# Winograd-style 3x3 convolution on one core: the first pair of images loaded by one transfer of 64 rows in place of two of 18 and 46

## The chip, the cores and the metric

The kernel runs on one core of a Trainium2 chip. The core's engines are TensorE (PE in the profile, with its weight loads as PEld), VectorE (DVE), ScalarE (ACT), GpSimd (POOL) and SyncE (SP); transfers between device memory and the on-chip memories run on 16 DMA engines that all queues share. The metric is the device time in microseconds; lower is better. It is the time of the whole kernel, from launch to the last byte stored.

## What is computed

The reference is a 3x3 convolution with padding 1 on 16 images of 64 channels and 64x64 pixels, to 128 channels, in float32:

```python
x_pad = np.pad(x, ((0, 0), (0, 0), (1, 1), (1, 1)))
for b in range(16):
    for co in range(128):
        for ci in range(64):
            for kh in range(3):
                for kw in range(3):
                    output[b, co] += weight[co, ci, kh, kw] * x_pad[b, ci, kh:kh+64, kw:kw+64]
```

The input has 16 MiB (16.8 MB), the output 32 MiB (33.6 MB).

## The kernel before, in words

Two images make a *pair*: their 2 x 64 channels fill the 128 partitions. There are eight pairs (`p`), and each is worked on in four blocks (`blk`) of eight row pairs. The kernel uses a trick along the height: for each pair of rows it needs the sum of the two input rows (`ss`, made by `sums` at L69), and the rows themselves in float16 (`xs`). In `group` (L142) TensorE accumulates in PSUM three results for each block, each for the two images (`b2`): `U`, from `ss` with the weights `G1`; `A`, from the odd rows and the row above, with the combined weights `G21` and `G0`; and `Bt`, from the even rows and the row below, with `G01` and `G2`. `U` is copied to SBUF by ACT (L156, tile `ut`); DVE adds it to `A` for the even output rows (L166) and to `Bt` for the odd output rows (L169) of the output tile `ot`. A block is 6 matmuls for `U` and 24 for `A` and `Bt`. PSUM has eight buffers of the tag `acc`, and a block takes six of them.

The loads go by three ways. SP issues, in this order and all at the start, the weights (L42), the first pair `x0` in float32 (two transfers, L46) and pairs 1 to 3 in float32 (`xf`, L50). These are on one queue, so their bytes flow in that order. POOL issues the loads of pairs 4 to 7 (L60), which convert to float16 on the way; the load of pair 4 comes after POOL's weight work (L88, L89), the others as buffers of `xs` come free.

The first pair is prepared like this (L91 to L93): in a loop over four cuts of its rows, DVE makes 8 of the 32 row sums per step (L69), and ACT casts 18, 16, 16 and 14 rows to float16 (L93). `keep` holds these instructions in program order on their engines, so DVE runs the four sums ahead of its first L166, and ACT the four casts ahead of its first L156. For the later pairs POOL makes the sums and ACT the casts (L161, pairs 1 to 3), a pair ahead of use.

The weights go another way: w_raw lands, POOL casts it (L54), TensorE transposes it by 18 small matmuls (L86), ACT copies the results to `Wt` (L87), and POOL makes the two combined weights (L88, L89).

The output tile of each image is stored whole, 2048 KB, at the end of its pair: that of the first image by SP's queue, that of the second by ACT's (held back in program order behind the next block's `ut` copies). The last pair alone is stored in two halves per image (L170), so that eighteen stores make up the output. `x0`, `xf` and `ot` share a pool of eight buffers.

Of the kernel before, what the change touches and what calls it, by code (L numbers as in the profile page):

```python
# [13 lines left out]
def kernel(  # L14
# [6 lines left out]
    nc = tc.nc  # L21
# [7 lines left out]
    x_rows = x.rearrange("b c h w -> (b c) h w")  # L29
# [12 lines left out]
    nc.sync.dma_start(w_raw, w_flat)  # L42
    x0 = opool.tile([128, H, W], F32, tag="ot", name="x0")
    cuts = [(0, 18), (18, 34), (34, 50), (50, 64)]
    for lo, hi in ((0, 18), (18, 64)):
        nc.sync.dma_start(x0[:, lo:hi, :], x_rows[0:128, lo:hi, :])  # L46
    xf = {}
    for p in (1, 2, 3):
        xf[p] = opool.tile([128, H, W], F32, tag="ot", name="xf")
# [53 lines left out]
    for p in range(NP):  # L103
# [8 lines left out]
        for blk in range(4):  # L112
# [58 lines left out]
            if blk in parts:  # L171
                lo, hi = parts[blk]
# [34 lines left out]
```

## Time and profile before

| what | value |
|---|---|
| three timed runs | 126.34, 126.49, 126.95 us (median 126.49) |
| the profiled execution's own time | 126.43 us |
| its span, from the first to the last instruction | 124.6 us |
| what lies around the span | 1.8 us |
| PE busy | 106.7 us, 86% of the span |
| DVE, ACT, POOL busy | 82.7, 51.9, 36.7 us |
| bytes moved by the DMA engines | 46.57 MB, mean 374 GB/s |
| read from device memory, written to it | 17.07 MB, 33.55 MB |

Times inside the profile are microseconds from the start of the span; an entry "7.92 4.91" starts at 7.92 and lasts 4.91. A group of instructions stands as line, engine, operation, output and inputs, and count. A DMA issue stands with its size and with the time from issue to landing. "SPq" and "ACTq" are the issues of transfers on SP's and on ACT's queue. The granted clock (PEclk) is 1.00 until the matmuls have ended. "DMA share" is the mean busy share of the 16 DMA engines; packets are booked where they start, so it can be a little over 1. A loading transfer that converts is counted in GB/s by the float16 bytes, half of those that it reads.

### The profile page before, as it was taken

To read this page: it belongs to the slowest core of one execution; us is meant where nothing else is said; L and a number is where in the kernel's file an instruction comes from. 1 tells how busy PE (TensorE), PEld (TensorE's weight loads), DVE (VectorE), ACT (ScalarE), POOL (GpSimd) and SP (SyncE) were. 2 spreads that over 40 slices of the span, in tenths; PEclk is the share of its full clock that TensorE was granted. 3 is DMA by queue.
4 is the path that set the end of the run, shared out by engine and by line. 5 is a ranking of instruction groups with operands and counts; after the bars stand their busy time and mean duration, and the time that the engine had idled before them with its cause. 6 is when DMAs were issued, how large, how long until landed. Compare 5 with 4: busy or idle time off the path is not lost.

```text
span 124.6 us, 2417 instructions
## 1 busy us (share of the span) xinstructions
PE 106.7 (86%) x978; PEld 57.5 (46%) x978; DVE 82.7 (66%) x132; ACT 51.9 (42%) x84; POOL 36.7 (29%) x27
## 2 busy tenths in 40 slices
PE   0489999999999999999999999999999999990000
PEld 0334555555555555555555555555555555540000
DVE  0016887877787787888777778777877787774000
ACT  4339569735983389333333333333333333330000
POOL 2280095195899103910058000850000000000000
PEclk9999999999999999999999999999999999999555
DMA  4999999999999999999999999999999999999992
GB/s 117 356 437 418 305 329 331 431 347 426 410 368 318 342 358 392 350 342 344 373 365 358 334 342 400 452 421 426 421 426 436 431 421 442 426 410 410 439 407 87
DMA packets 4042, 46.57 MB, mean 374 GB/s; under 512 B 448, under 2 KB 448, under 8 KB 704
## 3 DMA queue, kind: packets, MB, share of 16 engines
q1 hardware_dynamic: 2160, 25.46, 49.5%
q10 hardware_dynamic: 1296, 16.78, 31.7%
q0 software_dynamic: 576, 4.19, 16.1%
q8 instruction: 7, 0.11, 0.3%
q14 instruction: 3, 0.02, 0.0%
HBM read 17.07 MB, written 33.55 MB: 406 GB/s over the span
## 4 chain that ended last, share of the span: by engine, by line
PE 84%; DMA 4%; DVE 2%; issue 1%; DVEq 0%; SPq 0%
PE acc L142 84%; DMA x<-in_x_dram 4%; DVE ot L166 1%; DVE ss L69 1%; DVE ot L169 0%; DVEq L202 0%; SPq L42 0%; DVEq L166 0%
## 5 line engine op out<-in xcount | busy, mean ns | idle before, releaser
L142 PE MATMUL acc<-xs,Wt 64*128 64x504 f16 (+3 forms) x768 | 89.8, 380 | 0.0
L142 PEld LDWEIGHTS <-Wt 64*128 64x128 f16 x960 | 56.4, 96 | 49.8 <-issue 4.0
L156 ACT COPY ut<-acc 128x512 f32<-128x512 f32 x64 | 34.4, 589 | 53.0 <-issue 32.1
L166 DVE TENSOR_TENSOR ot<-acc,ut 128x512 f32<-128x512 f32 x64 | 41.2, 686 | 22.0 <-PE acc L142 18.2
L169 DVE TENSOR_TENSOR ot<-acc,ut 128x512 f32<-128x512 f32 x64 | 41.1, 684 | 0.0
L142 PE MATMUL acc<-ss,Wt 64*128 64x504 f16 (+1 forms) x192 | 27.2, 384 | 1.0 <-DVE ss L69 1.0
L69 POOL TENSOR_TENSOR ss<-xs 128x1024 f16<-128x1024 f16 x8 | 16.8, 2127 | 20.8 <-DMA xs<-in_x_dram 20.8
L69 POOL TENSOR_TENSOR ss<-xf 128x1024 f16<-128x1024 f32 x6 | 14.1, 2360 | 12.8 <-DMA xf<-in_x_dram 12.8
L161 ACT CAST xs<-xf 128x1024 f16<-128x1024 f32 x12 | 12.0, 1057 | 0.0
L69 DVE TENSOR_TENSOR ss<-x 128x512 f16<-128x512 f32 x4 | 2.6, 690 | 8.8 <-DMA x<-in_x_dram 8.8
L86 PE MATMUL wp<-ident,w 128*64 128x128 f16 x18 | 1.3, 328 | 4.4 <-POOL w L54 4.4
L93 ACT CAST xs<-x 128x1024 f16<-128x1024 f32 (+2 forms) x4 | 4.0, 1048 | 2.1 <-DMA x<-in_x_dram 2.1
L60 POOL DMA_DIRECT2D xs<-in_x_dram x4 | 2.4, 601 | 7.6 <-PE acc L142 7.6
L86 PEld LDWEIGHTS <-w 128*64 128x64 f16 x18 | 1.1, 209 | 4.4 <-POOL w L54 4.4
L87 ACT CAST Wt<-wp 128x384 f16<-128x384 f32 x3 | 1.2, 487 | 3.1 <-PE wp L86 3.1
L88 POOL TENSOR_TENSOR Wt<-Wt 128x384 f16<-128x384 f16 x1 | 1.4, 1387 | 1.7 <-ACT Wt L87 1.7
L87 ACT ACT_TABLE_LOAD x1 | 1.3, 1283 | 0.7 <-PEq L191 0.7
L54 POOL CAST w<-w_raw 128x576 f16<-128x576 f32 x1 | 0.7, 663 | 2.4 <-DMA w_raw<-in_weight_dram 2.4
L89 POOL TENSOR_TENSOR Wt<-Wt 128x384 f16<-128x384 f16 x1 | 0.9, 904 | 0.0
masks.py:199 POOL TENSOR_SCALAR_AFFINE_SELECT ident<-ident 128x128 f16<-128x128 f16 x1 | 0.3, 292 | 0.1
masks.py:197 POOL MEMSET ident<- 128x128 f16 x1 | 0.2, 204 | 0.3 <-POOLq L191 0.3
L191 POOL MEMSET const-float32-0.0<- 128x1 f32 x1 | 0.1, 98 | 0.2 <-issue 0.2
(3 smaller groups left out, 0.3 us busy)
## 6 DMA issues: line engine op xcount, KB each, us to landing
out_dram<-ot SPq DMA_DIRECT2D x7, 2048.0 KB, 22.3
out_dram<-ot ACTq DMA_DIRECT2D x7, 2048.0 KB, 18.5
xf<-in_x_dram SPq DMA_DIRECT2D x3, 2048.0 KB, 21.8
xs<-in_x_dram POOLq DMA_DIRECT2D x4, 1024.0 KB, 23.6
out_dram<-ot SPq DMA_DIRECT2D x2, 1024.0 KB, 11.3
out_dram<-ot ACTq DMA_DIRECT2D x2, 1024.0 KB, 11.2
x<-in_x_dram SPq DMA_DIRECT2D x1, 1472.0 KB, 7.8
x<-in_x_dram SPq DMA_DIRECT2D x1, 576.0 KB, 4.8
```

Source lines behind the costliest of these rows:

```text
L60: keep(nc.gpsimd.dma_start(xs[p], x_rows[128 * p : 128 * p + 128, :, :]))
L69: eng.tensor_add(ss[p][:, lo : lo + n, :], v[:, lo : lo + n, 0, :], v[:, lo : lo + n, 1, :])
L86: nc.tensor.matmul(wp[q : q + 64, k * CO : k * CO + CO], w16[:, t::9], ident)
L87: keep(nc.scalar.copy(wrow(g), wp[:, 0 : 3 * CO]))
L88: keep(nc.gpsimd.tensor_sub(wrow(G21), wrow(G2), wrow(G1)))
L89: keep(nc.gpsimd.tensor_sub(wrow(G01), wrow(G0), wrow(G1)))
L93: keep(nc.scalar.copy(xs[0][:, lo:hi, :], x0[:, lo:hi, :]))
L142: nc.tensor.matmul(tiles[b2][:, lo - j0 : hi - j0, c_lo:c_hi], Wt[p0 : p0 + 64, wi, kw, :], rhs, start=i == 0, stop=i == n - 1,)
L156: keep(nc.scalar.copy(ut, U[b2]))
L161: keep(nc.scalar.copy(xs[q][:, lo : lo + 16, :], xf[q][:, lo : lo + 16, :]))
L166: nc.vector.tensor_add(ots[b2][:, j0 : j0 + RB, 0, :], A[b2], us[b2])
L169: nc.vector.tensor_add(ots[b2][:, j0 : j0 + RB, 1, :], Bt[b2], us[b2])
```

## The change

The two transfers that load `x0`, of rows 0 to 17 and of rows 18 to 63, become one of all 64 rows. Nothing else is changed; the sums and casts of the first pair stay cut in four as before, but every one of them now waits for the one transfer. Behind the change all line numbers are smaller by one.

```diff
     nc.sync.dma_start(w_raw, w_flat)
     x0 = opool.tile([128, H, W], F32, tag="ot", name="x0")
     cuts = [(0, 18), (18, 34), (34, 50), (50, 64)]
-    for lo, hi in ((0, 18), (18, 64)):
-        nc.sync.dma_start(x0[:, lo:hi, :], x_rows[0:128, lo:hi, :])
+    nc.sync.dma_start(x0, x_rows[0:128, :, :])
     xf = {}
```

The engines' instructions are the same and in the same order; SP alone has one transfer fewer to issue (8,192 KB of loads in four transfers rather than five, behind the weights).

## The prediction

> **What bounds the kernel now.** I read the page first, for shares and the slices, then the chain that ended last, then the timeline of the first 16 us, then the transfers.
>
> ```profile
> span 124.6 us, 2417 instructions
> PE   0489999999999999999999999999999999990000
> DMA  4999999999999999999999999999999999999992
> PE 84%; DMA 4%; DVE 2%; issue 1%; DVEq 0%; SPq 0%
> ```
>
> Two resources are busy from end to end. PE works from slice 2 to slice 36, and the DMA engines from the start to the end. The chain, in order of time:
>
> ```profile
> 1.17 4.75 DMA x<-in_x_dram
> 5.95 0.70 DVE ss L69
> 6.69 104.25 PE acc L142 x948
> 112.28 0.59 DVEq L202
> 112.88 0.60 DVE ot L169
> ```
>
> By this chain the small first transfer of x0 (landed at 1.17 + 4.8 = 5.97) releases the first sum, that releases PE, and PE runs without a break to 110.9. But the chain stops at 113.5, and the span goes on for 11.1 us. In these only stores run, so the DMA queue has to be looked at for itself. First the busy share of the DMA engines and GB/s, the last two columns, in stretches of the span; then transfers by size and time to landing: the two of x0, the two stores of pair 5 (issued at 87.30 on SP, 87.90 on ACT), and the last store (issued at 113.51).
>
> ```profile
> 0.00:2.00 2.00, 0.00 (x0) 0.00 (x0) 0.00 (x0) 1.27 (x1) 0.70 (x6) 1.00 0.14 23
> 8.00:10.00 2.00, 2.00 (x14) 0.86 (x12) 0.55 (x1) 0.55 (x1) 0.92 (x2) 1.00 1.04 443
> 80.00:100.00 20.00, 20.00 (x190) 10.84 (x188) 15.79 (x27) 6.44 (x12) 2.64 (x2) 1.00 1.01 430
> 100.00:112.00 12.00, 12.00 (x114) 6.38 (x110) 9.24 (x16) 4.29 (x8) 0.00 (x0) 1.00 1.01 427
> 120.00:122.00 2.00, 0.00 (x0) 0.00 (x0) 0.00 (x0) 0.00 (x0) 0.00 (x0) 0.50 0.83 352
> 122.00:124.00 2.00, 0.00 (x0) 0.00 (x0) 0.00 (x0) 0.00 (x0) 0.00 (x0) 0.50 0.20 82
> ```
>
> ```profile
> x<-in_x_dram SPq DMA_DIRECT2D x1, 1472.0 KB, 7.8
> x<-in_x_dram SPq DMA_DIRECT2D x1, 576.0 KB, 4.8
> out_dram<-ot SPq DMA_DIRECT2D x1, 2048.0 KB, 16.8
> out_dram<-ot ACTq DMA_DIRECT2D x1, 2048.0 KB, 16.0
> out_dram<-ot ACTq DMA_DIRECT2D x1, 1024.0 KB, 10.2
> ```
>
> Pair 5's stores land at 104.1 and 103.9, though pair 6's are issued at 100.10 and 100.71. So when new stores come, old ones still fill the engines: the true bound is the DMA queue, and PE runs a few us ahead of it. What a later PE costs is what is over this backlog.
>
> **The change part by part.**
>
> *One issue fewer on SP.* An issue of x0 takes 0.42 us. The three xf issues behind it come that much earlier, but their bytes queue behind x0's: nothing, and if that cover were gone, a gain of 0.42.
>
> *Landing of x0.* The first use waits for 2048 KB instead of 576. Not later than the second transfer lands now, 1.6 + 7.8 = 9.4 (DVE and ACT take it at 9.46 and 9.45): the same bytes behind the same weights. Not earlier than 2.10 MB at the best rate, 443 GB/s, after the weights landed (0.73 + 2.9 = 3.6): 3.6 + 4.7 = 8.35. The 576 KB took 5.97 - 3.6 = 2.35 us, 251 GB/s, the 1472 KB 3.45 us, 437 GB/s; the slowness of the first part is either its short rows or the start itself, which the trace does not part. I take the middle, 8.9. The first sum moves from 5.95 to 8.9, so the first U matmul from 6.69 to 9.6: **2.95 us later** (2.4 to 3.5).
>
> ```profile
> 6.69 1.47 PE L142 MATMUL acc<-ss,Wt 64*128 64x512 f16 x6 [0.96 <-DVE ss L69]
> 7.92 4.91 PE L142 MATMUL acc<-xs,Wt 64*128 64x512 f16 x24
> 9.45 2.83 ACT L93 CAST xs<-x 128x1024 f16<-128x1024 f32 x3 [2.08 <-DMA x<-in_x_dram]
> 12.19 1.06 ACT L156 COPY ut<-acc 128x512 f32<-128x512 f32 x2
> 13.30 2.78 PE L142 MATMUL acc<-xs,Wt 64*128 64x512 f16 x24
> ```
>
> *What is queued behind the wait.* ACT: first cast 8.9 to 10.1 (1.17 us), the others (2.83) to 12.9, then the first L156, at 12.9 instead of 12.19. PE needs the first cut for A after U, at 9.6 + 1.3 = 10.9, and it is there at 10.1. DVE: four sums of 0.69 to 11.7, its first L166 after the ut copy, at 13.5 instead of 12.80. PE goes on meanwhile: block 0 takes six PSUM buffers, the next U the last two, and block 0 ends on PE only near 15.5. So ACT and DVE lose 0.7 us of a slack that stays; nothing of it reaches PE. POOL's weight work and its load of pair 4 (8.22) do not wait for x0. Cover gone (an eviction that holds PE): 0.7 more.
>
> *PE's slow start.* The first block takes 12.65 - 6.69 = 5.96 us, the next 15.89 - 12.65 = 3.24, at the same granted clock of 1.00; the first 24 matmuls on xs take 4.91 against 2.78. No wait explains it: PE has no idle time there. The loss is 2.72 us, and what ends it decides what the delay is worth. If the slow stretch belongs to the first block, it moves along: 2.95. If it ended at about 12.4 whatever PE did, only 12.4 - 9.6 = 2.8 us would be slow instead of 5.7, half of the difference saved: 2.95 - 1.45 = 1.5. If the transposes at 4.42 had helped it to an end and now, after a break of 3.9 us instead of 0.96, no longer do, it lasts 12.4 - 4.42 = 8.0 us from 9.6 and costs 1.15 more: 4.1. I take the first, the nearest to what the rows show, and keep 1.5 to 4.1.
>
> [...]
>
> *What the backlog takes.* PE, DVE and the store issues move by S = 2.95. For each store: had the queue been empty, how early could the end be? For pair 6's (100.10), 8192 KB of stores are left, 8.39 MB at 428 GB/s, the rate of the windows from 80 to 112: 19.6 us. From issue to data lie 1.0 us (weights issued at 0.73; a share of 0.14 in the first 2 us means data from 1.72). The tail, from the mean engine's end to the last landing at 113.51 + 10.2 = 123.7, is 1.6 now (shares after 120 add up to 2.06 us, so the mean engine ends at 122.1); after a pause that lets all 16 engines start together it may be 0.6. So the end is 100.10 + S + 1.0 + 19.6 + 0.6 to 1.6 = 121.3 to 122.3 + S, and the backlog absorbs 1.4 to 2.4 us. The landing of pair 5 bounds it from above: 104.0 - 101.1 = 2.9. I take 2.1. The stores of pair 0 (23.26) have more cover: the third xf lands at 31.4 now, and 2.10 MB of it at 430 GB/s after the second one's 24.3 last until 29.2, against 23.26 + 2.95 + 1.0 = 27.2. Load 6 must now wait for PE (pair 1 ends near 38 instead of 35.1, against an issue at 36.23), some 2 us; it lands at 36.23 + 27.4 = 63.6 now, and PE begins pair 6 at 86.3, with POOL's 4.2 us of sums between: covered by 18 us.
>
> *Sum.* 2.95 - 2.1 = +0.85 on the profiled 126.43: 127.3. The median of the runs shown, 126.49, is 0.06 above that execution; the forecast for the median is **127.3 us**, +0.7%, and its own range 126.7 to 128.4 (S from 2.4 to 3.5 with 2.1, and 2.95 with 1.4 and 2.9, and some of both).
>
> **Rivals.**
>
> 1. *Hidden.* The slow stretch ends at the old time (S = 1.5), or the backlog holds 2.9. Then DMA remains the bound everywhere; the time is 126.0 to 126.8. For it: the DMA share near 1 in every window. Against: the stretch followed PE's work in the only view there is.
> 2. *It passes in full.* If each store needs its successor early (the engines end pair 5 unevenly, and the fast ones idle from 101 on), or S is 4.1, the end moves by 2.0 to 4.1: 128.5 to 130.5, about 129.4 with S = 2.95 and no cover. Against: pair 5 landing 4 us after pair 6's issue.
> 3. *Faster.* One long transfer fills the queue's front better: x0 in 4.7 us instead of 2.35 + 3.45 = 5.8, so the whole DMA chain is 1.1 us shorter at most, 125.4, and half of that likely, 125.9. It decides only if S stays under about 1.3, since the end by the stores is 121.8 + S against 123.7 - 0.6. Against: 8.9 - 5.95 alone is 2.95.
>
> **How the numbers follow.** Forecast 0.58, hidden 0.22, in full 0.12, faster 0.08. A measurement of this kernel can tell about 0.5%, 0.63 us, from no change. Slower by more: most of the forecast (0.48; the rest of it lies within) and all of rival 2: 0.60. Faster by more: the better half of rival 3 and a little of rival 1: 0.08. Within: 0.32. The range, 125.9 to 128.9, takes in rival 1, the better part of rival 2 and the likely half of rival 3.
>
> **What would show it.** Right: one x transfer of 2048 KB landing near 8.5 to 9; the first L142 near 9.6 instead of 6.69; every later store issue later by about 2.95 (pair 6's near 103); a gap in the DMA share just before that, about 102 to 104; a time from last matmul to end shorter than now by 2. Wrong: store issues late by 3 with no gap (backlog larger), or a first block much shorter than 5.96 (rival 1), or much longer (rival 2).

## The result and the profile after

The changed kernel took 127.57 us (median of 22 runs) against 126.58 us for the kernel before beside it (22 runs). The ratio of the comparison is 1.0042, with a 95% interval of 1.0023 to 1.0062: slower, by less than the 0.5% that the prediction took as its bound, though the interval reaches past that. The changed kernel's times spread from 126.26 to 128.59, where those of the kernel before lie between 126.22 and 127.08; the ratio leaves out runs over 1.5% above a kernel's fastest, here six of the changed one, while the medians hold them all and stand 0.99 us (0.8%) apart. Two later comparisons on other chips gave 1.0083 [1.0049, 1.0118] (medians 128.26 and 126.80) and 1.0043 [1.0003, 1.0082] (medians 127.69 and 126.62).

The profiled execution of the changed kernel took 128.37 us, 0.8 above the median, so what it shows need not hold in full for the median execution; its span is 126.6 us. Its chain, in order of time (start, duration):

```profile
1.17 7.60 DMA x<-in_x_dram
8.80 0.70 DVE ss L68
9.55 103.26 PE acc L141 x948
114.16 0.60 DVEq L201
114.75 0.60 DVE ot L168
```

The one transfer of x0 lands at 8.77, the first sum starts at 8.80 instead of 5.95, and the first U matmul at 9.55 instead of 6.69: 2.86 us later. But PE's piece is 103.26 us long and not 104.25, so PE ends only 1.9 us later. The timeline of the start says where the 0.99 went:

```profile
8.80 3.88 ACT L92 CAST xs<-x 128x1152 f16<-128x1152 f32 x4 [2.59 <-DMA x<-in_x_dram]
9.55 1.47 PE L141 MATMUL acc<-ss,Wt 64*128 64x512 f16 x6 [3.92 <-DVE ss L68]
10.78 3.92 PE L141 MATMUL acc<-xs,Wt 64*128 64x512 f16 x24
12.59 1.06 ACT L155 COPY ut<-acc 128x512 f32<-128x512 f32 x2
14.52 0.83 PE L141 MATMUL acc<-ss,Wt 64*128 64x512 f16 x6
102.58 0.34 ACTq L97 DMA_DIRECT2D out_dram<-ot  x1
```

Block 0 takes 14.52 - 9.55 = 4.97 us on PE instead of 5.96: the slow stretch at PE's start ended earlier. The last line is the issue of pair 6's second store, at 102.58 instead of 100.71. In the kernel before the same line is:

```profile
100.71 0.34 ACTq L98 DMA_DIRECT2D out_dram<-ot  x1
```

So the shift that the stores see is S = 1.87 us. The DMA engines, in stretches (the last two columns are the mean busy share of the 16 engines, and GB/s):

```profile
100.00:102.00 2.00, 2.00 (x22) 1.16 (x20) 1.94 (x4) 0.10 (x1) 0.00 (x0) 1.00 0.67 279
102.00:104.00 2.00, 2.00 (x24) 1.09 (x20) 1.42 (x3) 0.97 (x2) 0.00 (x0) 1.00 0.75 320
104.00:106.00 2.00, 2.00 (x22) 1.10 (x20) 1.66 (x3) 0.93 (x2) 0.00 (x0) 1.00 1.14 483
122.00:124.00 2.00, 0.00 (x0) 0.00 (x0) 0.00 (x0) 0.00 (x0) 0.00 (x0) 0.50 0.32 135
124.00:126.00 2.00, 0.00 (x0) 0.00 (x0) 0.00 (x0) 0.00 (x0) 0.00 (x0) 0.50 0.04 16
```

The same stretches of the kernel before:

```profile
100.00:102.00 2.00, 2.00 (x22) 1.16 (x20) 1.42 (x4) 1.07 (x2) 0.00 (x0) 1.00 1.00 418
102.00:104.00 2.00, 2.00 (x22) 1.04 (x18) 1.79 (x3) 0.80 (x2) 0.00 (x0) 1.00 1.00 426
```

There the share between 100 and 104 was 1.00. Now the engines pause for 0.33 x 2 + 0.25 x 2 = 1.2 us on average, just before pair 6's stores begin to flow: the backlog of stores has run out. That is the gap that was forecast. Its place holds; what the end of the span shows (a share of 0.04 in the last window) was not forecast, and is taken up below.

### The profile page after: what moved, and what is told of

Read it like the earlier page. It is cut to its first block, busy times and chain, and to the rows that moved or that the text cites. A ratio compares the mean times of both kernels' runs of the same rounds, so it can differ in the third digit from the quotient of the medians.

```text
span 126.6 us, 2416 instructions
## 1 busy us (share of the span) xinstructions
PE 105.8 (84%) x978; PEld 57.2 (45%) x978; DVE 82.7 (65%) x132; ACT 52.0 (41%) x84; POOL 36.2 (29%) x27
## 4 chain that ended last, share of the span: by engine, by line
PE 82%; DMA 6%; DVE 2%; issue 1%; DVEq 0%; SPq 0%
PE acc L141 82%; DMA x<-in_x_dram 6%; DVE ot L165 1%; DVE ss L68 1%; DVE ot L168 0%; DVEq L201 0%; SPq L42 0%; DVEq L165 0%
## 5 line engine op out<-in xcount | busy, mean ns | idle before, releaser
L141 PE MATMUL acc<-xs,Wt 64*128 64x504 f16 (+3 forms) x768 | 88.8, 377 | 0.0
L165 DVE TENSOR_TENSOR ot<-acc,ut 128x512 f32<-128x512 f32 x64 | 41.2, 686 | 23.8 <-PE acc L141 21.5
```

Source lines behind the costliest of these rows:

```text
L141: nc.tensor.matmul(tiles[b2][:, lo - j0 : hi - j0, c_lo:c_hi], Wt[p0 : p0 + 64, wi, kw, :], rhs, start=i == 0, stop=i == n - 1,)
L165: nc.vector.tensor_add(ots[b2][:, j0 : j0 + RB, 0, :], A[b2], us[b2])
```

## The experiments

Two readings of each profile carry them: S, the issue of pair 6's second store less 100.71, and the time from that issue to the end of the span. In the table, "block 0" is PE's time from its first U to its second; S is the shift of the first U plus the change of block 0 (and, where matmuls are left out, those), to within 0.15 us. Each row shows one profiled execution; its time can lie above or below the median beside it.

| kernel | first U | block 0 | S | span | issue to end | median, us | kernel before beside it |
|---|---|---|---|---|---|---|---|
| before | 6.69 | 5.96 | 0 | 124.6 | 23.9 | 126.58 | - |
| before, less PE work | 7.37 | 5.41 | -1.35 | 124.8 | 25.4 | 126.64 | 126.76 |
| before, cut at row 34 | 7.54 | 4.77 | -0.35 | 125.1 | 24.7 | 126.46 | 126.76 |
| changed, PE kept at work | 9.50 | 3.16 | 0.16 | 124.7 | 23.8 | 126.64 | 126.76 |
| before, two sums later | 9.30 | 4.56 | 1.20 | 125.1 | 23.2 | 126.78 | 126.62 |
| changed, first profile | 9.55 | 4.97 | 1.87 | 126.6 | 24.0 | 127.57 | 126.58 |
| changed, third profile | 9.47 | 5.22 | 2.03 | 127.0 | 24.3 | 127.69 | 126.62 |
| changed, PE kept at work, three sums later | 11.61 | 3.15 | 2.10 | 125.6 | 22.8 | 127.74 | 126.62 |
| before, with the wait alone | 10.29 | 5.74 | 3.37 | 126.4 | 22.3 | 128.22 | 126.76 |
| changed, three sums later | 11.68 | 5.31 | 4.33 | 127.2 | 22.2 | 128.76 | 126.80 |
| changed, second profile | 11.44 | 5.73 | 4.51 | 127.4 | 22.2 | 128.26 | 126.80 |
| changed, six sums later | 13.97 | 5.90 | 7.21 | 130.1 | 22.2 | 130.97 | 126.62 |
| before, one store left out | 8.28 | 5.65 | 1.27 | 124.1 | 22.1 | 124.91 | 126.80 |
| changed, one store left out | 9.49 | 5.27 | 2.10 | 125.0 | 22.2 | 127.19 | 126.80 |

**The wait without the transfer.** The theory was that PE starts later, and that the queue of stores absorbs a part. The rival was that the shape of the transfer matters. Here both transfers stay, and the wait alone is added:

```diff
+    late = const.tile([128, 2, W], F16)
+    keep(nc.vector.tensor_copy(late[:, 0, :], x0[:, H - 1, :]))
+    keep(nc.scalar.copy(late[:, 1, :], x0[:, H - 1, :]))
     for n, (lo, hi) in enumerate(cuts):
```

> The kernel before, with its two transfers, but a small copy on VectorE and one on ScalarE read the last row of x0 ahead of the first sum and the first cast, so that the wait is that of the change and the transfers are not. Backlog theory (PE starts later by S, the queue of stores absorbs about 2): first U matmul near 10.3 instead of 6.69, S about 3.6 less what the slow stretch gives back; +0.8 to +1.8 against before, 127.4 to 128.4. Rival, that the shape of the transfer or an uneven DMA engine costs the time: no change, 126.3 to 126.8. Rival, that the delay passes in full: +3 or more.

128.22 us, ratio 1.0122 [1.0077, 1.0167]. The wait alone costs as much as the change, and more: the second of two transfers lands at 9.42, the single one at 8.77. So it is the wait that costs. The single transfer takes back 0.65 us of the landing. The rival of the transfer's shape falls as the main cause.

**Half of the delay.**

```diff
-    for lo, hi in ((0, 18), (18, 64)):
+    for lo, hi in ((0, 34), (34, 64)):
```

> The kernel before with the cuts of its two transfers at row 34 instead of 18 (1088 and 960 KB). Backlog theory: the first part lands near 6.8 to 7.1, the first U matmul is later by 1.0 to 1.3, all of it absorbed: no change, 126.3 to 126.7. Rival, that a delay of PE passes in full: +1.0 to +1.3, 127.5 to 127.9.

126.46 us, ratio 0.9985 [0.9962, 1.0007]: no change, as the backlog theory has it. The first part landed at 1.16 + 5.58 = 6.74 and the first U began at 7.54, 0.85 late. In its profile, though, block 0 was 1.19 shorter, so S was not positive there; the profile alone would prove little.

**A delay under the bound, put in by hand.** For that reason the kernel before was also run with two more sums, into a tile that nobody reads, ahead of the first (the runs with three and six sums add the same line to the changed kernel):

```diff
+    late = const.tile([128, RB, W], F16)
+    v0 = x0.rearrange("p (j i) c -> p j i c", i=2)
+    for _ in range(2):
+        keep(nc.vector.tensor_add(late, v0[:, 0:RB, 0, :], v0[:, 0:RB, 1, :]))
     for n, (lo, hi) in enumerate(cuts):
```

> The kernel before, its two transfers kept, with two more sums of 0.69 us on VectorE ahead of the first sum: PE starts 1.4 us later, a delay under the 1.7 that the profiles give as the bound. Backlog theory: the median is within 0.3 of the kernel before (126.5 to 127.0), a few runs with a late end of the slow stretch above it. Rival, that every delay passes: +1.4, about 128.1.

126.78 against 126.62, ratio 1.0019 [0.9993, 1.0045], with S at 1.20 in the profile:

```profile
9.30 1.46 PE L146 MATMUL acc<-ss,Wt 64*128 64x512 f16 x6 [3.72 <-DVE ss L69]
101.91 0.34 ACTq L102 DMA_DIRECT2D out_dram<-ot  x1
```

The first U was 2.6 us late, since each of the two sums took 1.28 us and not 0.69 (see the end). The delay is absorbed; the rival's 128.1 lies far above the interval.

**PE kept at work while it waits.** Nine more matmuls, result unused, in the time in which PE waits for x0:

```diff
+    busy = psum.tile([128, 512], F32, tag="acc", name="busy")
+    for k in range(9):
+        keep(nc.tensor.matmul(busy, ident, w16[:, 0:512]))
     keep(nc.gpsimd.tensor_sub(wrow(G21), wrow(G2), wrow(G1)))
```

> The changed kernel with nine extra 128x512 matmuls (of the weights with the identity, result unused) between the transposes of the weights and the first U, in the time in which PE waits for x0. Theory that the slow start of PE follows its activity: block 0 takes 3.3 to 3.6 us, not 5.0; S falls from 1.9 (the profile of the changed kernel) to about 0.2, so the stores are nearly on time and the DMA queue is the bound again: 126.0 to 126.5, and the spread of the runs falls to that of the kernel before (0.9 us) from 2.3. Rival, transfer shape or uneven DMA engine: stays at 127.0 to 127.8 with the same spread.

126.64 us, ratio 0.9986 [0.9967, 1.0004], and a spread from 126.34 to 126.95: the time of the kernel before (0.14 above the expected 126.0 to 126.5), with its narrow spread. Its PE timeline:

```profile
5.49 3.16 PE L89 MATMUL busy<-w,ident 128*128 128x512 f16 x9
9.50 0.82 PE L144 MATMUL acc<-ss,Wt 64*128 64x512 f16 x6 [0.86 <-DVE ss L68]
10.15 2.69 PE L144 MATMUL acc<-xs,Wt 64*128 64x512 f16 x24
12.66 0.83 PE L144 MATMUL acc<-ss,Wt 64*128 64x512 f16 x6
```

The first U is as late as in the changed kernel (9.50), but block 0 takes 3.16 us, the length of the blocks in the middle of the kernel. So work of PE ahead of the block takes the slow stretch away: behind 3.16 us of extra matmuls, which ended 0.86 us before the first U, it is gone from block 0, and they lie where PE has nothing else to do. The time since the start doesn't end it: without extra matmuls block 0 still takes 5.90 us where the first U begins at 13.97 (six sums later). That takes S from 1.87 to 0.16, and with S near zero the late landing costs nothing. It is also the strongest evidence against the transfer's shape: the same transfer, and no loss.

**Less work for PE in the kernel before.**

```diff
-            A = group([(G21, 1), (G0, -1)])
+            A = group([(G21, 1)] if p == 0 and blk > 0 else [(G21, 1), (G0, -1)])
```

> The kernel before without the G0 half of A in blocks 1 to 3 of pair 0 (18 pairs of matmuls left out; those odd rows of two images lack a term): PE and all later stores are 1.9 us earlier. Theory that the DMA queue bounds the kernel before: no change, 126.3 to 126.7. Rival, that PE bounds it: 124.5 to 124.9.

Six matmuls fewer in each of three blocks are 18 matmuls, not 18 pairs of them. 126.64 us, ratio 0.9991 [0.9967, 1.0015]; the stores are issued 1.35 us earlier, and the time stays. PE does not bound the kernel before, although the chain gives it 84% of the span.

**The backlog taken away.** One store of 2048 KB of pair 3 is left out, in both kernels, long before the place where the engines pause:

```diff
-                held.append((p, 1, ots[1], lo, hi))
+                if p != 3:
+                    held.append((p, 1, ots[1], lo, hi))
```

> The kernel before without the store of pair 3's second image (2048 KB of the output are not written). Backlog theory: the DMA queue has 4.9 us less to do, so it no longer bounds the end; the stores of pair 6 do, by PE: the 121.3 to 122.3 of the prediction with S = 0, against a last landing at 123.7, or 1.4 to 2.4 us less: 124.3 to 125.3. Theory that PE bounds the kernel before by itself: no change, 126.5.

> The changed kernel with the same store left out. Backlog theory: nothing absorbs PE's delay any more, so it stands above the cut kernel before by the whole shift of PE, 1.3 to 2.9 us by where the slow stretch ends, about 2.0: 126.3 to 127.3, hardly less than the changed kernel itself (127.5). Theory that the cost of the change lies in the DMA queue (a transfer's shape, an uneven engine): it is lower by the same amount as the cut kernel before, so only about 1.0 above it.

The cut kernel before took 124.91 us (0.9848 of the whole one, [0.9813, 0.9883]), the cut changed kernel 127.19. So without the backlog the change costs 2.28 us by the medians, where with it it costs 1.0 to 1.5. In the cut kernel before, and in the cut changed kernel below it, the engines stand still ahead of pair 6's stores:

```profile
98.00:100.00 2.00, 2.00 (x22) 1.15 (x18) 1.27 (x3) 1.07 (x2) 0.00 (x0) 1.00 0.55 229
100.00:102.00 2.00, 2.00 (x23) 1.17 (x20) 1.95 (x4) 0.69 (x2) 0.00 (x0) 1.00 0.00 0
102.00:104.00 2.00, 2.00 (x23) 1.11 (x19) 1.45 (x3) 0.38 (x1) 0.00 (x0) 1.00 0.93 393
```

```profile
100.00:101.00 1.00, 1.00 (x12) 0.58 (x10) 0.71 (x2) 0.04 (x1) 0.00 (x0) 1.00 0.08 16
101.00:102.00 1.00, 1.00 (x14) 0.57 (x10) 1.00 (x2) 0.00 (x0) 0.00 (x0) 1.00 0.00 0
102.00:103.00 1.00, 1.00 (x14) 0.55 (x11) 0.78 (x2) 0.87 (x2) 0.00 (x0) 1.00 0.00 0
103.00:104.00 1.00, 1.00 (x14) 0.53 (x12) 0.62 (x2) 0.21 (x1) 0.00 (x0) 1.00 1.23 524
```

One part of the expectation missed: the cut changed kernel was not "hardly less" than the changed kernel but 1.07 us less than it on the same chip (127.19 against 128.26). So a part of the changed kernel's time lies in the DMA queue after all: 1.07 us by this comparison, in which the changed kernel's median is the highest of the three (127.57 and 127.69 in the others). The profiles say the same: with S at 2.10 the cut changed kernel ends 22.2 us after the issue, where the whole one with S at 1.87 and 2.03 ends 24.0 and 24.3 us after it (below).

**More delay.** With three sums, then six, ahead of the first sum of the changed kernel:

> The changed kernel with three more sums of 0.69 us on VectorE (into a tile that nobody reads) between the landing of x0 and the first sum: PE starts 2.1 us later still, at 11.6. Backlog theory, with the backlog already used up: the whole 2.1 on top of the changed kernel, 129.4 to 129.9. Theory that delays are absorbed in part anywhere: 128.0 to 128.6.

> The changed kernel with six more sums of 0.69 us on VectorE between the landing of x0 and the first sum, 4.1 us in all. Backlog theory, as sharpened by the profiles so far (the span ends 22.2 us after the issue of pair 6's second store wherever the DMA engines paused before it): 4.1 above the changed kernel on the same chip, 131 to 132.5, and the span ends 22.0 to 22.4 after that issue. Rival, that a part of each further delay is taken up somewhere, as the run with three sums (0.5 above the changed kernel beside it, not 2.1) could mean: 129 to 130.5.

128.76 and 130.97 us, the first below its expectation of 129.4, the second just under its 131. Beside the changed kernel on the same chips (128.26 and 127.69) that is 0.5 and 3.3 us more, for 2.07 and 4.14 us of delay: by the medians, less than the theory had. By the profiles the rule holds: S is 4.33 and 7.21, and the span ends 22.2 us after the issue both times, with these issues:

```profile
105.04 0.34 ACTq L101 DMA_DIRECT2D out_dram<-ot  x1
107.92 0.34 ACTq L101 DMA_DIRECT2D out_dram<-ot  x1
```

Between the two delayed kernels the step is 2.2 us for 2.07. So the changed kernel stands above the line of these two by up to one microsecond, rather than they below it. The next run stands above it too.

**Both at once.** Fourteen matmuls to keep PE at work, and the three sums:

> The changed kernel with both: fourteen extra matmuls that keep PE at work until shortly before the first U, and three extra sums that delay it by 2.1. Block 0 then takes 3.3 us in any run, and S is about 2.3. Backlog theory: 0.6 above the kernel before, 127.0 to 127.6. If the spread of the changed kernel's runs (2.3 to 2.6 us) comes from the end of the slow stretch, it falls under 1.2 here; if from the landing of x0 or from uneven DMA engines, it stays.

127.74 us, ratio 1.0074 [1.0041, 1.0107], from 126.87 to 129.55. Block 0 took 3.15 us, and S was 2.10. The median is a little above the expectation, and the span ends 22.8 us after the issue, 0.6 later than in the delayed kernels: with S near 2, just above the backlog, this kernel costs 1.1 us as the changed one does, and not only the 0.4 that S leaves over the backlog. The spread did not fall: it is 2.7 us with the slow stretch gone from the profile. So the runs can spread as widely without it; what spreads them is not shown.

**The changed kernel again.**

> The changed kernel once more, beside the others on one chip, for a second profile: 127.2 to 127.9. If one DMA engine that ends alone is what sets the time, as in the first profile (its last 2 us have a DMA share of about one sixteenth), the profile shows it again and the shift of PE does not explain the time; if the shift of PE does, the last landing follows the issue of pair 6's stores by the same 23 us as in the kernel with the wait alone.

> The changed kernel beside these on the same chip: 127.2 to 128.3; span 22.0 to 22.4 after the issue of pair 6's second store if no engine ends alone, and S between 1.8 and 4.5.

128.26 us, above the expectation of 127.2 to 127.9, and 127.69 us, inside its own. The profiled executions took 129.14 and 128.74 us; like the first (128.37), they stand 0.8 to 1.1 us above their medians. The three profiles of one kernel differ in two ways. In the second, the transfer of x0 landed at 10.67 instead of 8.77, S was 4.51, and the end came 22.2 us after the issue, as in the delayed kernels:

```profile
1.16 9.51 DMA x<-in_x_dram
10.70 0.70 DVE ss L68
11.44 104.02 PE acc L141 x948
```

In the first and the third, S was 1.87 and 2.03, which by the rule of 22.2 gives a span of 124.8 and 124.9; they ended 24.0 and 24.3 us after the issue, 1.8 and 2.1 later. The windows of the third profile at its end:

```profile
122.00:123.00 1.00, 0.00 (x0) 0.00 (x0) 0.00 (x0) 0.00 (x0) 0.00 (x0) 0.50 0.53 221
123.00:124.00 1.00, 0.00 (x0) 0.00 (x0) 0.00 (x0) 0.00 (x0) 0.00 (x0) 0.50 0.08 33
124.00:125.00 1.00, 0.00 (x0) 0.00 (x0) 0.00 (x0) 0.00 (x0) 0.00 (x0) 0.50 0.06 25
125.00:126.00 1.00, 0.00 (x0) 0.00 (x0) 0.00 (x0) 0.00 (x0) 0.00 (x0) 0.50 0.04 16
```

A share of 0.06 is one engine of sixteen, and 25 GB/s is what one engine moves: in the first profile each of the last packets of data has 8 KB and takes 0.31 us, some 26.5 GB/s. So in the third profile no more than one engine's work is left in the window from 124, and less in the next, and the kernel waits for it; in the first profile two engines are left at the end, and one alone for the last 1.0 us. In the runs at 22.1 to 22.3 the share has such values for less time (with three sums 0.78 from 124 to 125, then 0.06 and 0.00; in the second profile 0.93, then 0.09 and 0.00). That a pause before pair 6's stores lets a late engine catch up would explain those with a long pause, but not the run with the wait alone, which ends at 22.3:

```profile
100.00:102.00 2.00, 2.00 (x22) 1.09 (x20) 1.27 (x3) 1.07 (x2) 0.00 (x0) 1.00 0.94 401
102.00:104.00 2.00, 2.00 (x22) 1.11 (x20) 2.00 (x4) 0.59 (x2) 0.00 (x0) 1.00 0.59 246
104.00:106.00 2.00, 2.00 (x22) 1.15 (x20) 1.42 (x4) 0.48 (x1) 0.00 (x0) 1.00 0.99 418
```

Its pause, about 1 us on average, is no longer than the 1.2 us of the first profile. Why one engine is so late in the first and third profile, and not in the kernel before or in the one with PE kept at work (which ends by the same stores and uses the same transfer), is open: no run was made that sets it apart.

## Why the prediction was right, and where not

The prediction said 127.3 us, slower by 0.7%, range 125.9 to 128.9; the medians are 127.57 to 128.26 over the three comparisons, and the ratio 1.0042 (+0.5 us) lies toward the small end of its own range for the likeliest case. By its steps:

- *One issue fewer on SP, nothing.* Right; the xf issues came 0.47 us earlier (1.64 instead of 2.11), and the first xf is taken only 0.20 us earlier (POOL's first sum at 15.56 instead of 15.76), without effect on PE, whose start is the landing of x0.
- *Landing of x0 at 8.9, between 8.35 and 9.4.* 8.77 in the first profile and 8.7 to 9.0 in the others but one; there it was 10.67, which lies outside the bounds. The row that would have warned of it was not in the one profile that was there: in the cut kernel before, the 576 KB landed at 7.4 instead of 5.97.
- *First U 2.95 us later.* 2.86.
- *What is queued behind the wait, nothing.* Right: the first ut copy was at 12.59 (forecast 12.9), the first L165 on DVE at 13.49 (13.5), and PE ran through.
- *The slow stretch moves along with PE (S = 2.95).* This is the term that was mis-sized. Block 0 took 4.97, 5.22 and 5.73 us in the three profiles, not 5.96, and between 4.56 and 5.96 over all runs without extra matmuls and with all their work. S was 1.87 and 2.03 where x0 landed on time. The upper bound (4.1) and the lower (1.5) both held for these. Why block 0 differs from run to run is not shown. That it depends on PE's work ahead of it is shown by the two kernels with extra matmuls: it took 3.16 us behind 3.16 us of them, and 3.15 behind 4.24.
- *The backlog absorbs 2.1, between 1.4 and 2.4.* From the profiles it is 124.6 - (100.71 + 22.2) = 1.7. Right within its bounds. That a delay under it was free is shown by the run with two sums (126.78 against 126.62), that those above it were not by the ones with three and six (128.76 and 130.97).
- *The sum.* With the measured terms, 2.0 - 1.7 = +0.3, not +0.85. The ratio has +0.5 and the medians +1.0, so 0.2 to 0.7 us are not in these terms. In two of the three profiled executions an engine ends late, and the span ends 1.8 and 2.1 us past the rule of 22.2, which the prediction did not have as a term; it spoke of uneven engines only as a tail of 0.6 to 1.6 us and in rival 2. But these executions are slower than the median by 0.8 and 1.05 us, and no profile of a median one was taken, so that the same tail, only shorter, makes up the rest is likely and not shown. The direction and the mechanism, a delay less a backlog, were right. That the number came out so near is in part luck: a shift too large by about 0.9 and a backlog too large by 0.4 left +0.85 where the terms as measured give +0.3, and something that the sum lacked made up for it.
- *The sign at the end.* The time from the last matmul to the end was to be shorter by 2. It was 13.7 us before, and 13.8 and 14.0 in the first and third profile; only in the second, at 11.9, did it come. This sign failed where the late engine set the end.

Rival 1 (hidden) had the right sign in its first step, a slow stretch that ends earlier, and the lowest of the runs, 126.26, is as it has it. Rival 2 (in full): the whole delay passes only where the backlog is taken away (2.28 us). Its other condition, a shift of 4.1, came about in the second profile with S at 4.51, by a late landing and not by the slow stretch; that execution took 129.14 us, inside the rival's 128.5 to 130.5. Rival 3 (faster) was refuted where it had its best chance: with PE kept at work S is 0.16, under its limit of 1.3, and the time is 126.64 against 126.76, a ratio of 0.9986 [0.9967, 1.0004], not 0.5 to 1.1 us less.

## What to carry to other kernels

When the DMA engines are busy from end to end, as here (a share of 1.01 from 80 to 112), find the store whose issue comes closest to their running dry. Here a delay cost what it had over the backlog at that store, 1.7 us, by the profiles with a large one (1.8 us of the span for S = 3.37, 5.5 for 7.21), and the chain of waits does not show it. Near the backlog's own size the changed kernel's cost was larger than that, 0.5 to 1.0 us for a shift of 2.0, and in its first and third profile the DMA engines did not end together. The wait for the whole of the transfer in place of its first rows cost PE's start the landing of the rest, 2.86 us; the backlog took 1.7 of it, and all of it was free once TensorE was kept at work in the meantime (126.64 us against 126.76). The runs of the changed kernel spread over 2.3 us where those of the kernel before spread over 0.9, so look at all the runs, not at one ratio or one profile.

## What the runs showed of the hardware that was not expected

A sum of VectorE over rows of the first pair took 0.69 us alone, and 1.28 us in two profiles (less PE work, two sums later) where a subtraction of POOL for the weights had started before it. This is the kernel before with less PE work, where POOL was first by 0.18 us:

```profile
5.85 0.91 POOL L88 TENSOR_TENSOR Wt<-Wt 128x384 f16<-128x384 f16 x1 [1.65 <-ACT Wt L87]
6.03 1.28 DVE L69 TENSOR_TENSOR ss<-x 128x512 f16<-128x512 f32 x1 [6.03 <-DMA x<-in_x_dram]
6.72 1.36 POOL L89 TENSOR_TENSOR Wt<-Wt 128x384 f16<-128x384 f16 x1
```

In the profile of the kernel before, VectorE was first, by 0.07 us (5.95 against 6.02): its sum took 0.69, and POOL's subtraction 1.39 instead of 0.91. So in each of these two profiles the one that started first kept its time, 0.91 or 0.69 us, and the other took 0.5 to 0.6 us longer than 0.69 or 0.91; why, no run shows. The 0.6 us are most of the step in PE's start from 6.69 in the kernel before to 7.37 here, and the time of both is the same; the changed kernel's sums start after POOL's weight work (8.80 against its end at 7.69 in the first profile) and do not meet it.

The granted clock was 1.00 in the slow block as in the next (6.69 to 12.65 and 12.65 to 15.89 in the kernel before), so that column did not show the slow start; only the time of the same 24 matmuls did, 2.69 us with PE kept at work against 3.92 in the changed kernel and 4.91 in the kernel before.
